# A conformer and attention layer: layer norm on rows between two sets of transposes, and softmax sums spread over partitions on chip

## The chip, the cores and the metric

The kernel runs on one core of a Trainium2 chip. Its engines are PE (TensorE, the matmuls), DVE (VectorE), ACT (ScalarE), POOL (GpSimd) and SP (SyncE, which here issues every DMA, one after the other). The metric is the device time of one execution in microseconds. Lower is better.

## The reference, cut to what matters

One layer is computed for 2048 prompt tokens and 32 tokens of running streams, all in fp32. Two parts of it matter here: the layer norm of the convolution branch, which takes a mean and a variance over the 512 channels of one token, and the softmax's division by the sum of its row.

```python
glu = a * jax.nn.sigmoid(b)
y = conv1d_depthwise(glu, conv_w) + conv_b        # width 31, causal, 512 channels
mu = mean(y, -1); var = mean((y - mu)**2, -1)     # per token
y = (y - mu) * rsqrt(var + EPS) * ln_g + ln_b     # ln_g, ln_b per channel
y_conv = silu(y) * silu(gate_c)
...
s = (q_nope @ k_nope.T + q_rope @ k_rope.T) * ATT_SCALE   # 8 heads, masked by chunks of 64
p = softmax(s, -1)
y_att = (p @ v) * silu(gate_a)                            # 64 channels a head
mixed = concat([y_conv, y_att], -1) @ w_out
return x + rmsnorm(mixed, g_post)
```

## The kernel before, in words

**Stages.** The program has three stages. Stage A (to about 507 us) brings x in, norms and transposes it and runs the input projection in two halves of 1024 tokens; half 1 carries the 32 stream tokens too. Every product is made of three matmuls, because each fp32 operand is split into a high and a low part (`emit_chunk`, L359 to L361: `xh,wh`, `xl,wh`, `xh,wl`; POOL makes the low part `wl` of each weight block at L156, and the raw blocks `wraw` are loaded on SP's queue). The convolution's 31 taps run beside it on DVE (L381) and on POOL with ACT. Stage B (to about 1090 us) is attention, stage C the output projection and the stream tokens' attention. Half 0's layer norm falls to the middle of stage A, between the two halves; half 1's falls to the start of stage B.

**Layout.** The result of the convolution, `acc`, lies with channels on partitions: 4 tiles of 128 channels by the tokens. A token's mean and variance run over partitions and tiles.

**Layer norm before.** For 128 tokens PE transposes four 128x128 blocks of `acc` into a PSUM tile `tp` (L198 in half 0, L1388 in half 1), DVE takes mean and variance of each row (L178, L179), and POOL turns the variance into 1/sqrt (L142, L143). The result `bmv` has two numbers a token, tokens on partitions. But `acc` has tokens along its rows, so each partition needs all tokens' numbers: SP stores `bmv` to DRAM (`st_d`, L185), and, after that has landed, loads it into all 128 partitions (`z<-st_d`, L187). Then two operations subtract and multiply (L193 on DVE for half 0, L149 on POOL for half 1). Half 0 ends with `emit_mix`: for each of the four channel tiles a Silu over 1024 tokens on ACT (L208), a gate load of 512 KB, a product on POOL and a store to `mix_d`. There are 8 such token tiles in half 0 and 9 in half 1 (the ninth has 32 rows).

**Softmax sums before.** The product of the unnormalised weights with v comes out as `yp`, channels (two heads of 64) on partitions. The reciprocal sums `rl` (L1163, L1164 on DVE) have queries on partitions. For each of 32 pairs of heads and 256 queries, `store_rl` stores the two heads' sums to DRAM (`rl_d`, L1280, 256 numbers of 4 B each), loads the gate (`gat`, L1288), and loads the sums back, each head's over 64 partitions (`rlb<-rl_d`, L1291, twice); POOL multiplies `gat` by `rlb`, then `yp` by `gat`, and the result goes to `mix_d` (L1306).

**What sets the order.** In stage A the Tile framework's scheduler orders what the program emits; the layer norm's steps are handed to a background queue (`later`, `bg`) with a cost of `LC` = 3 each, and `queue_ln` puts the second step of a tile `LL` = 2 tiles behind its first. In stage B a planner in the program keeps a clock for each engine (`hold`, `after`, `tps` for the PSUM tiles `tp`, with `DL` = 10 us assumed for a DMA) and writes the order of PE, ACT, DVE and POOL; that order is kept. SP's order is the scheduler's throughout. Each engine takes its instructions strictly in its order, and SP too: a DMA that must wait for another keeps all later ones waiting. Also on SP's queue in stage B are the stores and loads that stage k and v through DRAM (`k_d<-lng`, `v_d<-lng` from the staging tiles `lng` and `stgw`, which ACT fills from PSUM at L834; PE's products into `tp` for them are at L880) and the rotary tables (`tab`, L1022, used by DVE at L1053). PE's lines in attention are L1117 to L1119 (scores `sps`), L1202 to L1208 (transposes of the weights `pc`), L1253 to L1256 (`ops`, weights with v); `ql` is the low part of the queries, made by POOL at L156.

Of the kernel before, what the change touches and what calls it, by code (L numbers as in the profile page):

```python
# [88 lines left out]
def hybrid_stream_step(ctx: ExitStack, tc: tile.TileContext, a: dict, o: dict):  # L89
# [24 lines left out]
    rl_d = dram.tile([NH, SEQ], F32, name="rl_d")  # L114
# [46 lines left out]
    lnp = conv_ctx.enter_context(tc.tile_pool(name="lnp", bufs=4, side="left"))  # L161
# [3 lines left out]
    zs = {}  # L165
# [8 lines left out]
    def ln_stats(t, ps, r):  # L174
# [6 lines left out]
        return mv  # L181

    def ln_spread(t, mv, r):
        rows = st_d[t * P:t * P + r]
# [3 lines left out]
        return z  # L188

    def ln_apply(z, c0, r, subtract, multiply):  # L190
        x = acc[:, :, c0:c0 + r]
        for tt, op, q in ((subtract, ALU.subtract, 0), (multiply, ALU.mult, 1)):
            tt(x, x, z[:, :r, q].unsqueeze(1).broadcast_to([P, CT, r]), op)  # L193

    def emit_ln(t, c0, r):
        ps = ln_pool["ps"].tile([P, 512], F32, name="tp")
        for i in range(CT):
            nc.tensor.transpose(ps[:r, i * P:(i + 1) * P], acc[:, i, c0:c0 + r], ident)  # L198
        zs[t] = ln_spread(t, ln_stats(t, ps, r), r)

    def emit_ln2(t, c0, r):
        ln_apply(zs.pop(t), c0, r, nc.vector.tensor_tensor, nc.vector.tensor_tensor)

    def emit_mix(i, t0, n):
        g = lnp.tile([P, HALF + DEC], F32, name="lng", bufs=1)
        nc.sync.dma_start(out=g[:, :n], in_=gate_d[i, :, t0:t0 + n])
        y = acc[:, i, :n]
        nc.scalar.activation(y, y, AF.Silu, bias=col(LN_B, i), scale=col(LN_G, i))  # L208
        pool_tt(y, y, g[:, :n], ALU.mult)
        nc.sync.dma_start(out=mix_d[i, :, t0:t0 + n], in_=y)  # L210

    with ExitStack() as pa:
# [295 lines left out]
        for half in range(2):  # L508
# [77 lines left out]
            if half == 0:  # L586
                queue_ln([(j, j * P, P) for j in range(8)])
# [14 lines left out]
            for n, key in enumerate(seq2[:8 - len(lastpair)]):  # L602
# [7 lines left out]
                if half == 0 and n == CT - 1:  # L610
                    for i in range(CT):
                        later(lambda i=i: emit_mix(i, 0, HALF), LC)
            if lastpair:
# [7 lines left out]
                for ci, (c0, m) in enumerate(chunks):  # L621
# [5 lines left out]
                    if ci == 0:  # L627
                        transpose_x(range(8, 12), 0, fill=True)
# [11 lines left out]
    with ExitStack() as pb:  # L640
# [40 lines left out]
        def load_wkv():  # L681
            raw = lnp.tile([P, HALF + DEC], F32, name="lng", bufs=1)[:, 0:NH * P].rearrange("p (h c) -> p h c", h=NH)
# [140 lines left out]
        spare = lnp.tile([P, HALF + DEC], F32, name="lng", bufs=1)  # L823
        stgw = wk.tile([P, 1024], F32, name="stgw", bufs=1)
        stgs = [stgw[:, i * 512:(i + 1) * 512] for i in range(2)]
        stgs += [spare[:, i * 512:(i + 1) * 512] for i in range(2)]
# [244 lines left out]
        rows, rls = {}, {}  # L1071
# [28 lines left out]
        def s_run(ready):  # L1100
# [6 lines left out]
            if c == 0:  # L1107
                if j == 0:
                    rls[(h, g)] = small.tile([P, 2], F32, name="rl2", bufs=12)
                rt = small.tile([P, 8], F32, name="row", bufs=RB)  # L1110
                rows[(h, g, j)] = {"mx": rt[:, 0:4], "ls": rt[:, 4:8], "rl": rls[(h, g)][:, j:j + 1], "p": {}}
# [35 lines left out]
        def e_run(ready):  # L1147
# [10 lines left out]
            if c == ns - 1:  # L1158
                def total(ready):
# [6 lines left out]
                    if j:  # L1166
                        store_rl(h, g)
# [108 lines left out]
        def store_rl(h, g):  # L1276
            ts = slice(g * 256, (g + 1) * 256)

            def put(ready):
                nc.sync.dma_start(out=rl_d[h, ts].rearrange("(j p) -> p j", p=P), in_=rls.pop((h, g)))  # L1280
                t = hold("sp", 0.4, ready) + DL
                if h % 2:
# [495 lines left out]
```

## Time and profile before

| | |
|---|---|
| median of three runs | 1310.7 us (1310.13 to 1317.46) |
| the profiled execution | 1310.61 us, its span 1308.8 us |
| PE busy | 1232.9 us, 94% of the span |
| DVE, ACT, POOL busy | 883.0, 749.2, 627.2 us |
| granted PE clock, mean | 0.974 |
| DMA, mean | 95 GB/s, 42.2% of the 16 engines' time |

PE has little idle time in all, but it is not spread evenly: it lies where stages meet. A row of a view reads: start or total, length, engine, line of the kernel, operation, output<-inputs, and in brackets the idle time before it with the instruction or DMA that ended it. The granted clock is a share of full speed: 1.00 is 2.4 GHz, and a mean between .5 and 1 is a mix of 1.2 and 2.4 GHz.

### The profile page before, as it was taken

Reading aid. Unit: us, or ns where it says so; the run is one execution under the profiler, and the core shown is the slowest. Engines: PE = TensorE matmul, PEld = TensorE weight load, DVE = VectorE, ACT = ScalarE, POOL = GpSimd, SP = SyncE. Lnnn points to the kernel's source line nnn. Section 1 sums busy time; section 2 is a strip of 40 time slices with the busy share of each in tenths; the row PEclk is TensorE's granted clock in tenths of the full one; section 3 lists DMA queues with packets and bytes.
Section 4 is the critical chain, followed back from the end, with each engine's and each line's share of the span. In section 5 each row is a group of like instructions: output and inputs, shape, how many; then the busy total and the mean of one; then the engine's idle time right before and its main releaser. Section 6 shows DMA issues by size and latency. Waiting matters only on the chain.

```text
span 1308.8 us, 20918 instructions
## 1 busy us (share of the span) xinstructions
PE 1232.9 (94%) x7272; PEld 1100.1 (84%) x7272; DVE 883.0 (67%) x1814; ACT 749.2 (57%) x1748; POOL 627.2 (48%) x680
## 2 busy tenths in 40 slices
PE   7999999699999998868996999999999999999997
PEld 6889987589899997757896999999999998788876
DVE  4299898255997913646684888898988884543333
ACT  5366722155565223656685888888888884345221
POOL 5299942136999322545554434545554365111110
PEclk8999999899899999989998999999999999999999
DMA  8122253223313323596666323355245356944332
GB/s 294 31 72 80 79 140 105 56 57 109 113 49 87 113 83 91 107 117 123 115 76 92 37 44 43 76 58 63 46 79 47 39 90 132 284 156 144 95 109 69
DMA packets 166606, 124.23 MB, mean 95 GB/s; under 512 B 67031, under 2 KB 148489, under 8 KB 166499
## 3 DMA queue, kind: packets, MB, share of 16 engines
q1 hardware_dynamic: 166339, 122.82, 42.2%
q8 instruction: 57, 0.93, 0.4%
q14 instruction: 50, 0.41, 0.3%
q10 hardware_dynamic: 160, 0.07, 0.0%
HBM read 83.64 MB, written 39.21 MB: 94 GB/s over the span
## 4 chain that ended last, share of the span: by engine, by line
PE 71%; DMA 13%; DVE 6%; POOL 5%; ACT 3%; issue 2%; SPq 1%; POOLq 0%; DVEq 0%; ACTq 0%
PE mm L361 7%; PE mm L360 7%; PE mm L359 7%; PE sps L1117 4%; PE sps L1119 4%; PE sps L1118 4%; DMA st_d<-bmv 3%; PE ops L1255 2%; PE yx L1710 2%; PE yx L1711 2%; PE yx L1709 2%; DVE cv L381 2%; PE sps L1711 2%; PE sps L1710 2%; PE sps L1709 2%; PE mm L441 2%
## 5 line engine op out<-in xcount | busy, mean ns | idle before, releaser
L381 DVE SCALAR_TENSOR_TENSOR cv<-glu,cwT,cv 128x1024 f32<-128x1024 f32 x186 | 239.7, 1289 | 6.0
L1154 ACT ACTIVATE pc<-pc,row 128x512 f32<-128x512 f32 (+3 forms) x320 | 210.2, 659 | 34.3 <-DVE pc L1133 33.6
L360 PE MATMUL mm<-xl,wh 128*128 128x352 f32 (+1 forms) x584 | 209.2, 358 | 2.6 <-DVE xl L347 2.5
L361 PE MATMUL mm<-xh,wl 128*128 128x352 f32 (+1 forms) x584 | 208.0, 356 | 3.2 <-POOL wl L156 3.2
L359 PE MATMUL mm<-xh,wh 128*128 128x352 f32 (+1 forms) x584 | 208.0, 358 | 0.3 <-ACT xh L331 0.3
L1224 DVE TENSOR_TENSOR ptl<-tp,pth 128x512 fp32r<-128x512 f32 (+1 forms) x288 | 187.8, 656 | 28.9 <-ACT pth L1220 26.2
L1220 ACT CAST pth<-tp 128x512 fp32r<-128x512 f32 (+1 forms) x288 | 159.9, 558 | 35.0 <-PE tp L1208 24.7
L1133 DVE TENSOR_SCALAR_CACHE_REDUCE pc<-sps,row 128x512 f32<-128x512 f32 (+2 forms) x192 | 125.7, 655 | 21.8 <-PE sps L1119 14.6
L1117 PE MATMUL sps<-kh,qh 128*128 128x512 f32 (+3 forms) x320 | 132.8, 415 | 4.0 <-DVE pc L1133 2.6
L360 PEld LDWEIGHTS mm<-xl,wh 128*128 128x128 f32 x584 | 112.2, 192 | 13.8 <-DVE xl L347 3.9
L361 PEld LDWEIGHTS mm<-xh,wl 128*128 128x128 f32 x584 | 112.3, 192 | 13.3 <-POOL wl L156 3.5
L1119 PE MATMUL sps<-kh,ql 128*128 128x512 f32 (+3 forms) x320 | 116.7, 365 | 6.6 <-POOL ql L156 6.6
L359 PEld LDWEIGHTS mm<-xh,wh 128*128 128x128 f32 x584 | 112.4, 193 | 10.9 <-ACT xh L331 0.6
L149 POOL TENSOR_TENSOR acc<-acc,ptap 128x512 f32<-128x512 f32 x92 | 118.7, 1306 | 4.6 <-ACT acc L386 2.7
L1118 PE MATMUL sps<-kl,qh 128*128 128x512 f32 (+3 forms) x320 | 116.1, 363 | 0.0
L156 POOL TENSOR_TENSOR wl<-wraw,wh 128x1024 fp32r<-128x1024 f32 x27 | 64.9, 2403 | 97.6 <-ACT wh L155 97.5
L156 POOL TENSOR_TENSOR ql<-qf,qh 128x256 fp32r<-128x256 f32 x64 | 46.9, 735 | 114.0 <-ACT qh L155 98.8
L1255 PE MATMUL ops<-ptl,vb 128*128 128x256 f32 x288 | 85.9, 298 | 5.6 <-DVE rl L1163 4.4
L1253 PE MATMUL ops<-pth,vb 128*128 128x256 f32 x288 | 88.2, 306 | 2.2 <-ACT pth L1220 2.2
L149 POOL TENSOR_TENSOR yp<-yp,low 64x256 f32<-64x256 f32 x64 | 46.9, 734 | 89.2 <-ACT low L1264 88.1
L1133 DVE TENSOR_SCALAR_CACHE_REDUCE pc<-sps 128x512 f32<-128x512 f32 (+3 forms) x128 | 80.0, 628 | 12.8 <-PE sps L1119 11.2
L1202 PE MATMUL tp<-ident,pc 128*128 128x128 f32 x288 | 80.3, 279 | 6.6 <-ACT lng L834 4.9
(386 smaller groups left out, 3265.2 us busy)
## 6 DMA issues: line engine op xcount, KB each, us to landing
wraw<-in_w_in SPq DMA_DIRECT2D x31, 512.0 KB
xr<-in_x_prompt SPq DMA_DIRECT2D x16, 512.0 KB
out_y_p<-src SPq DMA_DIRECT2D x32, 256.0 KB
mix<-mix_d SPq DMA_DIRECT2D x7, 1024.0 KB
gate_d<-gt SPq DMA_DIRECT2D x24, 176.0 KB
xt<-in_x_prompt SPq DMA_DIRECT2D x8, 512.0 KB
gate_d<-gt SPq DMA_DIRECT2D x16, 256.0 KB
gat<-gate_d SPq DMA_DIRECT2D x32, 128.0 KB
```

The source lines that it names most:

```text
L149: nc.gpsimd.tensor_tensor(dst, x, y, op)
L359: nc.tensor.matmul(ps[:, :n], wh[:, k], rh, start=(k == 0), stop=False)
L360: nc.tensor.matmul(ps[:, :n], wh[:, k], rl, start=False, stop=False)
L361: nc.tensor.matmul(ps[:, :n], wl[:, k], rh, start=False, stop=(k == KT - 1))
L381: nc.vector.scalar_tensor_tensor(box["ps"], x, cw(j), box["ps"], ALU.mult, ALU.add)
L1117: nc.tensor.matmul(d, qh[:, qs], kh[b][:, ks], start=True, stop=False)
L1118: nc.tensor.matmul(d, qh[:, qs], kl[b][:, ks], start=False, stop=False)
L1119: nc.tensor.matmul(d, ql[:, qs], kh[b][:, ks], start=False, stop=True)
L1133: nc.vector.tensor_scalar(p_[:, :m], d, -SCALE, r["mx"][:, c - 1:c] if c else None, ALU.mult, ALU.min, accum_out=r["mx"][:, c:c + 1])
L1154: nc.scalar.activation(p_, p_, AF.Exp, bias=r["mx"][:, ns - 1:ns], scale=-1.0, accum_out=r["ls"][:, c:c + 1])
L1220: nc.scalar.copy(out=ph[:, :nn], in_=ps[:, :nn])
L1224: nc.vector.tensor_tensor(pl[:, :nn], ps[:, :nn], ph[:, :nn].bitcast(F32), ALU.subtract)
```

## The change

**Layer norm.** The tile's rows in PSUM, tokens on partitions, are normed right there: a DVE `tensor_scalar` reads `tp` and subtracts and multiplies with the row's own two numbers, into the place of the tile in `acc`, now as rows. Four more transposes (`ln_back`, L196 after) bring it back to channels on partitions in a second `tp` tile. From there half 0 goes through Silu on ACT straight from PSUM (four of 128x128 a tile, in place of four of 128x1024 for all), a POOL product of 128x512 with a gate tile of two slots, and one store a tile; half 1 goes through one ACT copy of 128x512 and the store. `st_d` and `z` are gone: 17 stores and 17 loads. `queue_ln` is now called after half 0's gates, and not ahead of its latents, a tile's second step stands ahead of the next one's first, and the transposes of x for tiles 8 to 11 take their PSUM from `mm`, not from `tp`.

**Softmax sums.** The sums of two heads and 256 queries are gathered in one tile `rlt`. POOL widens them to 128x256 (each sum copied 64 times along the row), PE transposes that in two 128x128 pieces (L1296), so that the sums lie along rows on the right partitions, and DVE multiplies them from PSUM with the gate (L1300). POOL's product with `yp` is as before. Gone are 64 stores `rl_d`, 64 loads `rlb` and 32 products on POOL.

```diff
 def queue_ln(jobs):
     for i in range(len(jobs) + LL):
+        if i >= LL:
+            later(lambda a=jobs[i - LL]: emit_ln2(*a), LC)
         if i < len(jobs):
             later(lambda a=jobs[i]: emit_ln(*a), LC)
-        if i >= LL:
-            later(lambda a=jobs[i - LL]: emit_ln2(*a), LC)
...
-def ln_spread(t, mv, r):
-    nc.sync.dma_start(out=rows, in_=mv[:r])
-    z = lnp.tile([P, P, 2], F32, name="z")
-    nc.sync.dma_start(out=z[:, :r], in_=rows.partition_broadcast(P))
-def ln_apply(z, c0, r, subtract, multiply):
...
+def ln_rows(ps, c0, r):
     nc.vector.bn_stats(st[:r], ps[:r])
     nc.vector.bn_aggr(mv[:r], st[:r])
     rsqrt_eps(mv[:r, 1:2], mv[:r, 1:2], 1)
+    x = ln_x(c0, r)
+    nc.vector.tensor_scalar(x, ps[:r].rearrange("p (k c) -> p k c", k=CT), mv[:r, 0:1], mv[:r, 1:2],
+                            ALU.subtract, ALU.mult)
+def ln_back(ps, c0, r):
+    x = ln_x(c0, r)
+    for i in range(CT):
+        nc.tensor.transpose(ps[:, i * P:i * P + r], x[:, i], ident[:r, :r])
...
-            if half == 0:
-                queue_ln([(j, j * P, P) for j in range(8)])
             latents(half, tiles)
...
-                    for i in range(CT):
-                        later(lambda i=i: emit_mix(i, 0, HALF), LC)
+                    queue_ln([(j, j * P, P) for j in range(8)])
...
-                        transpose_x(range(8, 12), 0, fill=True)
+                        transpose_x(range(8, 12), 0, mm, fill=True)
...
-            nc.sync.dma_start(out=rl_d[h, ts].rearrange("(j p) -> p j", p=P), in_=rls.pop((h, g)))
-                nc.sync.dma_start(out=rb[i * VD:(i + 1) * VD], in_=rl_d[h - 1 + i, ts].partition_broadcast(VD))
+                pool_copy(rb, rlt[h // 2 % 2][:, g].unsqueeze(3).broadcast_to([P, 2, 2, VD]))
+                nc.tensor.transpose(ps[:, j * P:(j + 1) * P], rb[:, j], ident)
-                pool_tt(gt, gt, rb, ALU.mult)
+                nc.vector.tensor_tensor(gt, ps[:, 0:256], gt, ALU.mult)
```

On DVE, at the third layer-norm tile of half 0 and the transposed x that follows (`xl`), the order before is:

```order
61 L193 TENSOR_TENSOR acc<-acc,z 128x4x128 [waits DMAHW2_49]
62 L193 TENSOR_TENSOR acc<-acc,z 128x4x128 [waits DVE_49]
63 L178 BN_STATS bst<-tp 128x6 [waits PE_49]
64 L193 TENSOR_TENSOR acc<-acc,z 128x4x128 [waits DMAHW4_49]
65 L179 BN_AGGR bmv<-bst 128x2 [waits DVE_49]
66 L193 TENSOR_TENSOR acc<-acc,z 128x4x128 [waits DVE_49]
67 L332 SCALAR_TENSOR_TENSOR xl<-tp,cols,xh 128x512 [waits Activation_49]
```

and now, from the first tile on:

```order
56 L182 BN_STATS bst<-tp 128x6 [waits PE_49]
57 L183 BN_AGGR bmv<-bst 128x2 [waits DVE_49]
58 L186 TENSOR_SCALAR acc<-tp,bmv 128x4x128 [waits DVE_49,Pool_49]
59 L182 BN_STATS bst<-tp 128x6 [waits PE_49]
60 L183 BN_AGGR bmv<-bst 128x2 [waits DVE_49]
61 L333 SCALAR_TENSOR_TENSOR xl<-mm,cols,xh 128x512 [waits Activation_49]
62 L186 TENSOR_SCALAR acc<-tp,bmv 128x4x128 [waits DVE_49,Pool_49]
63 L333 SCALAR_TENSOR_TENSOR xl<-mm,cols,xh 128x512 [waits Activation_49] x3
```

The two operations with `z`, each pair behind a DMA, have become one operation behind POOL's 1/sqrt, in a chain of DVE and POOL alone.

On SP, early in attention, between the load of a block of latents (`src<-ckv_d`) and the staging stores that follow it, the order before is:

```order
222 L185 DMA st_d<-bmv 128x2 [waits DMAHW4_49,DVE_49,Pool_49]
223 L774 DMA src<-ckv_d 128x4x128 [waits DMAHW5_49,PE_49]
224 L187 DMA z<-st_d 128x256 [waits DMAHW6_49,DMAHW4_49]
225 L1280 DMA rl_d<-rl_4762 128x2x1 [waits DMAHW7_49,DVE_49]
226 L775 DMA src<-kr_d 128x4x64 [waits DMAHW0_49]
227 L860 DMA k_d<-lng 128x512 [waits DMAHW1_49,Activation_49]
228 L782 DMA src<-qn_d 128x4x256 [waits DMAHW2_49,PE_49]
229 L185 DMA st_d<-bmv 128x2 [waits DMAHW3_49,DVE_49,Pool_49]
230 L886 DMA v_d<-lng 128x512 [waits Activation_49]
```

and at the same loads now:

```order
209 L772 DMA src<-ckv_d 128x4x128 [waits DMAHW5_49,PE_49]
210 L773 DMA src<-kr_d 128x4x64 [waits DMAHW6_49]
211 L1412 DMA mix_d<-acc 128x4x128 [waits DMAHW7_49,Activation_49]
212 L857 DMA k_d<-lng 128x512 [waits DMAHW0_49,Activation_49]
213 L780 DMA src<-qn_d 128x4x256 [waits DMAHW1_49,PE_49]
214 L883 DMA v_d<-lng 128x512 [waits DMAHW2_49,Activation_49]
```

The rows with `st_d`, `z` and `rl_d` are gone from between the loads and `k_d`, and a store `mix_d<-acc`, which waits for ACT, stands there.

On PE, in attention, at the same scores of one unit (`sps`, 384 keys) and the same products with v, the order before is:

```order
3957 L1205 MATMUL tp<-ident,pc_6315 128x128
3958 L1117 MATMUL sps_4391<-kh_4421,qh 128x384 [waits DVE_49]
3959 L1118 MATMUL sps_4391<-kl_4423,qh 128x384
3960 L1119 MATMUL sps_4391<-kh_4421,ql 128x384
3961 L1253 MATMUL ops_4458<-pth,vb_4424 128x256 [waits Activation_49]
3962 L1254 MATMUL ops_4458<-pth,vb_4424 128x256
```

and now:

```order
4010 L1201 MATMUL tp<-ident,pc_4471 128x128
4011 L1113 MATMUL sps_4435<-kh_4465,qh 128x384 [waits DVE_49]
4012 L1114 MATMUL sps_4435<-kl_4467,qh 128x384
4013 L1115 MATMUL sps_4435<-kh_4465,ql 128x384
4014 L1296 MATMUL tp<-ident,rlb 128x128 [waits PE_49,Pool_49]
4015 L1296 MATMUL tp<-ident,rlb 128x128
4016 L1249 MATMUL ops_4502<-pth,vb_4468 128x256 [waits Activation_49]
4017 L1250 MATMUL ops_4502<-pth,vb_4468 128x256
```

The two transposes of the widened sums `rlb` stand between them, and wait for POOL. Of the 32 pairs of them 8 stand in the part of the order that belongs to attention's start (to 725 us in the trace before), the other 24 behind it.

## Rows read from the trace of the kernel before

**Rows 1.** By stage: length, PE, PEld, DVE, ACT, POOL busy us, clock, DMA share, GB/s

```profile
215.00:345.00 130.00, 110.53 (x608) 100.31 (x608) 70.38 (x91) 51.97 (x85) 60.17 (x56) 0.91 0.32 87
505.00:725.00 220.00, 182.24 (x1147) 159.64 (x1146) 136.54 (x399) 139.45 (x345) 112.36 (x157) 0.94 0.64 104
725.00:1080.00 355.00, 353.89 (x2570) 332.73 (x2569) 313.24 (x969) 304.96 (x805) 170.14 (x183) 1.00 0.41 57
```

**Rows 2.** Waits of PE from 215 to 345 us: total, times, longest us

```profile
PE tp L330 <- DVE xl L332: 5.6, 2, 3.8
PE tp L330 <- DVE bst L178: 5.4, 2, 3.1
PE mm L361 <- POOL wl L156: 3.2, 1, 3.2
```

**Rows 3.** Waits of DVE from 215 to 345 us

```profile
DVE acc L193 <- DMA z<-st_d: 41.9, 7, 8.5
```

**Rows 4.** Waits of SP's queue from 215 to 345 us

```profile
SPq L187 <- DMA st_d<-bmv: 28.5, 7, 6.7
```

**Rows 5.** Waits of PE from 505 to 725 us

```profile
PE sps L1119 <- POOL ql L156: 6.6, 2, 5.2
PE tp L1202 <- ACT lng L834: 4.9, 3, 4.2
PE ops L1255 <- DVE rl L1163: 4.4, 1, 4.4
PE tp L880 <- ACT lng L834: 4.3, 1, 4.3
PE tp L880 <- ACT stgw L834: 2.4, 2, 1.2
```

**Rows 6.** SP's instructions in order of time, around 550 us

```profile
543.43 0.37 SPq L774 DMA_DIRECT2D src<-ckv_d  x1
552.00 0.32 SPq L187 DMA_DIRECT2D z<-st_d  x1
553.40 0.45 SPq L860 DMA_DIRECT2D k_d<-lng  x1
```

**Rows 7.** PE's in order of time, around 565 us: start, length, [idle before]

```profile
565.38 0.47 PE L1202 MATMUL tp<-ident,pc 128*128 128x128 f32 x1 [4.24 <-ACT lng L834]
```

**Rows 8.** 20 us of the attention's start, columns as in the first group

```profile
560.00:580.00 20.00, 11.18 (x55) 8.85 (x55) 6.08 (x22) 9.41 (x25) 8.57 (x15) 0.74 0.80 145
```

**Rows 9.** PE's in order of time, around 227 us

```profile
226.39 0.39 PE L361 MATMUL mm<-xh,wl 128*128 128x512 f32 x1
226.62 0.60 PE L198 MATMUL tp<-ident,acc 128*128 128x128 f32 x4
226.98 0.47 PE L359 MATMUL mm<-xh,wh 128*128 128x512 f32 x1
227.29 0.39 PE L360 MATMUL mm<-xl,wh 128*128 128x512 f32 x1
```

**Rows 10.** PE's in order of time, around 802 us

```profile
801.68 0.27 PE L1202 MATMUL tp<-ident,pc 128*128 128x128 f32 x1
...
802.00 0.27 PE L1208 MATMUL tp<-ident,pc 128*128 128x128 f32 x1
```

**Rows 11.** Groups by line and form: busy us, mean ns | idle before

```profile
L1053 DVE TENSOR_TENSOR qf<-tp,tab 128x256 f32<-128x256 f32 x62 | 26.2, 423 | 30.0 <-DMA tab<-in_rope_q 10.7 <-POOL ql L156 6.6 <-PE tp L1046 4.6
L149 POOL TENSOR_TENSOR gat<-gat,rlb 128x256 f32<-128x256 f32 x32 | 24.6, 770 | 32.0 <-DMA gat<-gate_d 17.1 <-DMA rlb<-rl_d 9.1 <-issue 5.8
L156 POOL TENSOR_TENSOR wl<-wraw,wh 128x1024 fp32r<-128x1024 f32 x27 | 64.9, 2403 | 97.6 <-ACT wh L155 97.5
L834 ACT COPY lng<-tp 128x512 f32<-128x512 f32 x16 | 9.4, 589 | 14.4 <-DMA k_d<-lng 8.4 <-DMA v_d<-lng 3.4 <-PE tp L856 1.8
```

**Rows 12.** POOL's in order of time, around 582 us

```profile
581.95 0.23 POOL L142 TENSOR_SCALAR bmv<-bmv 128x1 f32<-128x1 f32 x1 [0.70 <-DVE bmv L179]
582.26 0.57 POOL L143 TENSOR_TENSOR bmv<-bmv,nhalf 128x1 f32<-128x1 f32 x1
```

More of the change, by code (lines that the diff above doesn't have):

```diff
@@ L681, in load_wkv @@
         def load_wkv():
-            raw = lnp.tile([P, HALF + DEC], F32, name="lng", bufs=1)[:, 0:NH * P].rearrange("p (h c) -> p h c", h=NH)
+            raw = lng[:, 0:NH * P].rearrange("p (h c) -> p h c", h=NH)
             nc.sync.dma_start(out=raw, in_=w_kvb.rearrange("p (h c) -> p h c", h=NH))
@@ L821, in prep_tasks @@
                     (lambda: latest(box["t2"], tps.ready()), query(1))]
-        spare = lnp.tile([P, HALF + DEC], F32, name="lng", bufs=1)
         stgw = wk.tile([P, 1024], F32, name="stgw", bufs=1)
         stgs = [stgw[:, i * 512:(i + 1) * 512] for i in range(2)]
-        stgs += [spare[:, i * 512:(i + 1) * 512] for i in range(2)]
+        stgs += [lng[:, i * 512:(i + 1) * 512] for i in range(2)]
         stg = Slots(len(stgs))
@@ L1070, in hybrid_stream_step @@
         banks, pcs, gats = Slots(NB), Slots(NP), Slots(2)
-        rows, rls = {}, {}
+        rows = {}
+        rlt = [small.tile([P, 8, 2, 2], F32, name=f"rlt{i}", bufs=1) for i in range(2)]
         exp_q = []
@@ L1274, in pv_run, with scale_rows @@
                 after("act", PE_["ot"], t, out)
[L1276 removed]
+        def scale_rows(h, g):
             ts = slice(g * 256, (g + 1) * 256)
[L1279 to L1283 removed]
+            if h % 2 == 0:
+                return
             def load(ready):
@@ L1307, in save @@
                     done[("mix", h, g)] = hold("sp", 0.4, ready) + DL
-                after("pool", PE_["gate"], t, scale)
-            after("sp", PE_["gate"], latest(done[("rl", h, g, 0)], done[("rl", h, g, 1)]), put)
+                after("dve", PE_["gate"], t, scale)
+            after("sp", PE_["gate"], lambda: gats.ready(), load)
         q_list = list(range(len(units)))
@@ L1386, in l_run, with back, out @@
             ps = tp.tile([P, 512], F32, name="tp")
-            for i in range(CT):
-                nc.tensor.transpose(ps[:r, i * P:(i + 1) * P], acc[:, i, c0:c0 + r], ident)
+            ln_turn(ps, c0, r)
             te = hold("pe", t_pe(256, 4), ready)
-            zk = zslots.take()
             def stats(ready):
-                mv = ln_stats(t, ps, r)
-                te = hold("dve", t_dve(512) + 0.1, ready)
+                ln_rows(ps, c0, r)
+                te = hold("dve", t_dve(512) + 0.2, ready)
+                te = hold("pool", 0.3, te)
+                te = hold("dve", t_dve(512), te)
                 tps.give(kslot, te)
-                te = hold("pool", 0.3, te)
-                z = ln_spread(t, mv, r)
-                def norm(ready):
-                    ln_apply(z, c0, r, pool_tt, pool_tt)
-                    te = hold("pool", 2.4, ready)
-                    zslots.give(zk, te)
+                after("pe", PE_["l"], lambda: latest(te, tps.ready()), back)
+            def back(ready):
+                k = tps.take()
+                ps = tp.tile([P, 512], F32, name="tp")
+                ln_back(ps, c0, r)
+                te = hold("pe", t_pe(256, 4), ready)
+                def out(ready):
+                    nc.scalar.copy(out=acc[:, :, c0:c0 + r], in_=ps.rearrange("p (k t) -> p k t", k=CT)[:, :, 0:r])
+                    te = hold("act", t_act(512), ready)
+                    tps.give(k, te)
                     nc.sync.dma_start(out=mix_d[0:CT, :, HALF + c0:HALF + c0 + r].rearrange("k p t -> p k t"),
```

71 lines of the change are left out of this document (37 added, 34 removed).

## The prediction

> **What bounds the kernel now.** I read the busy times by stage first, then the waits of PE in the stages where it idles, then followed each wait back to the engine or queue that caused it. PE is busy for 94% of the span, so time can be won only where PE is not busy or where its clock is low, and every instruction that is added to PE elsewhere costs its full length. [Rows 1] say where: from 215 to 345 us, where the halves of stage A meet, PE is busy for 110.53 of 130 us, at a mean clock of 0.91; from 505 to 725 us, the start of attention, for 182.24 of 220 at 0.94; from 725 to 1080 us for 353.89 of 355 at 1.00.
>
> So the two stages offer 130.00 - 110.53 = 19.5 us and 220.00 - 182.24 = 37.8 us of idle time. The clock adds to it. A mean of 0.91 between 1.2 and 2.4 GHz is 18% of 130 us at the lower level, 23.4 us; PE is busy for 85% of the stage, and half of that is lost: 23.4 x 0.85 / 2 = 9.9 us. In attention's start 12% of 220 us is 26.4 us, and x 0.83 / 2 = 10.9 us. The fall of the clock goes with the idle time: in the emptiest 20 us PE is busy for 11.18 us at 0.74 [rows 8]. Together 29.4 us at the boundary and 48.7 us at the start.
>
> What PE waits for at the boundary is DVE: 5.6 and 5.4 us for the low part of the transposed x and for the statistics [rows 2], and DVE itself stood for 41.9 us, seven times, before operations with `z` [rows 3], whose load SP could issue only when the store of `bmv` had landed (28.5 us of SP's queue) [rows 4]. The 3.2 us for POOL's `wl` are of another kind. At attention's start the five largest waits of PE make 22.6 us [rows 5]. One of them can be followed through: SP issues a load at 543.43, stands behind `st_d` until it issues `z` at 552.00, and only then, at 553.40, the store `k_d<-lng` [rows 6]; ACT can't refill `lng` before that store has landed, and PE stands 4.24 us until 565.38 for ACT's copy [rows 7]. The other waits for `lng` and `stgw` are of this form; those for `ql` and `rl` hang on tables and gate loads that SP issued late, behind `rlb`.
>
> **The change, part by part.** *The layer norm's round trips*, 17 stores and 17 loads, go, and with them the 41.9 us of DVE. Of the 14.2 us of PE's waits in [rows 2], 3.2 stay with POOL; so about 70% of the 29.4 us, 20 us, is what could be won at the boundary. I take 18, since the new operation on DVE still waits, now for POOL's 1/sqrt, and behind it stand the statistics of the next tile and the `xl` that PE needs. The trace has no such wait, but its parts: in attention POOL begins as DVE's result comes and is done 0.9 us later (581.95 to 582.83) [rows 12]; at the boundary it can stand behind one `wl` of 2.4 us [rows 11]. Eight tiles make 8 x 0.9 = 7 us to 8 x (0.9 + 2.4) = 26 us of DVE's waiting, against 41.9. With all 26, two fifths of the gain stay, 18 x (1 - 26/41.9) = 7 us: that is the lower bound, and I take the value nearer to 0.9, the measured row.
>
> *Transposes added to the layer norm.* At 226.62 four of them run; the next two matmuls start 0.36 and 0.31 us later, and matmuls of 128x512 follow each other by 0.23 ahead of them [rows 9]: 0.36 + 0.08 = 0.44 us for four. Half 0 adds 8 x 0.44 = 3.5 us, half 1 adds 9 x 0.44 = 4.0.
>
> *Work of the others at the boundary.* DVE loses one of two operations a tile, POOL none that counts (four products of 128x1024 become eight of 128x512), SP's half-0 stores become eight of a tile. They wait for POOL's product, and the next raw weights stand behind them on SP; PE's margin there is the weights' lead, and the 3.2 us for `wl` may grow. I leave it at zero in the sum, with 0 to +6 us (two waits of 3.2) for the range. That x's transposes take PSUM from the ring of the projection can cost PE a wait for an eviction, or win one; it is in the same bounds.
>
> *Attention's start.* `z` and `rl_d`, `rlb` leave SP's queue. The 22.6 us of [rows 5] needn't vanish: staging through DRAM stays, the store `mix_d<-acc` now stands ahead of `k_d` and waits for ACT, which must first copy a tile (0.59 us each by the copies to `lng`, 9 x 0.59 = 5.3 us more on ACT, which is not full) [rows 11]. I take three quarters, 17 us, and of the clock the same share as of the idle time, 10.9 x 17 / 37.8 = 4.9: 22 us. Against it stand the 4.0 us of half 1's transposes and 8 of the 32 pairs that spread the sums. A transpose follows the one before by 0.32 / 3 = 0.107 us [rows 10], so a pair is 0.21 us, and 8 make 1.7.
>
> *The rest of attention.* The other 24 pairs are 24 x 0.21 = 5.1 us on a PE that has 1.1 us to spare [rows 1]: full price. That SP no longer stands for `rl_d` there wins nothing, since PE doesn't idle for it. DVE takes over the product with the gate at 0.42 us (by `qf`, which also reads PSUM [rows 11]), 24 x 0.42 = 10 us on top of 313 of 355: no bound yet. POOL gives up 0.77 us and takes a widening copy of similar size. The 17.1 us that POOL waited for `gat` [rows 11] become DVE's, if they stay; DVE makes weights that PE waits for, so here the bounds are 0 and +6 us (a third of 17.1). I take 0, because the gate load no longer stands behind `rl_d`.
>
> Sum: boundary -18 + 3.5 = -14.5; start -22 + 4.0 + 1.7 = -16.3; rest +5.1. That is -25.7 on the profiled 1310.6 us, which is the median of the runs too (1310.7): **1285 us**.
>
> **The rivals.** *The transfers are late anyway.* The DMA engines are busy for 0.80 of the emptiest 20 us [rows 8] and for 0.64 of the whole start [rows 1]. If their load, and not SP's blocked queue, makes the staged tiles late, only the waits for `ql` and `rl` behind the tables and the gate go, three quarters of 6.6 + 4.4 = 11.0, 8 us: start -8 + 5.7 = -2.3, and in all -14.5 - 2.3 + 5.1 = -11.7, 1299 us. With the lower bound at the boundary as well (-7 + 3.5) it is -0.7, 1310. For it: the load. Against it: the 8.6 us between two issues in [rows 6], which no load of the engines explains. The Trainium skill, "DMA: Bandwidth & Descriptors", section "Issuing engines are not separate DMA queues", says that all DMAs end up on the same 16 engines; that speaks for this rival, and no row here tells how much of the busy share is the many small packets that leave.
>
> *New waits on PE: the slower side.* PE gets 17 + 32 = 49 places at which its strict order waits for a chain of DVE and POOL that was not in its way before: 1/sqrt or widening on POOL, with its operations of 0.7 to 2.4 us. If PE stood there for 0.9 us each time (POOL's part in [rows 12]), it would lose 44 us, and the time would be 1285 + 44 = 1329. It breaks even at 25.7 / 49 = 0.52 us a place, and is slower by 1% from 0.79 us. Against it: PE waits today on POOL's `ql` at every unit, and from 725 to 1080 us it idles for 1.1 us in all, with POOL busy for less than half of the time [rows 1]; the back transposes stand a tile or more behind.
>
> *All of it is won.* If the boundary's 20 us and nine tenths of the start's 48.7 go, it is -20 + 3.5 - 44 + 5.7 + 5.1 = -50, 1261 us. Against it: attention's start also has to load its first k and v through DRAM, whoever issues.
>
> *The transposes run at the lower clock.* From 725 to 1080 us, where transposes of the weights stand between all products, the granted clock is 1.00 [rows 1], and they follow each other by 0.107 us [rows 10]. If the added ones brought the clock down around themselves, their 14.3 us would count twice: 1285 + 14 = 1299. The Trainium skill, "TensorE: Matmul & The Clock Gate", section "Part 4: PE-mode transpose", says that a transpose doesn't count as busy for the clock; this trace speaks against an effect of it here.
>
> **How the numbers follow.** A measurement of this kernel tells about 1% from no change, so the bounds are 1297.6 and 1323.8 us. My forecast, with a spread of some 12 us from its two recovered terms, has 0.50; all of it won 0.10; transfers late anyway 0.25; lower clock 0.03; new waits on PE 0.12. Faster by over 1% is the forecast and the full gain with a little of the third, 0.63; within 1% most of the third, the fourth and a little of the slower side, 0.27; slower 0.10. The range must hold 8 in 10: it reaches from 1264, near the full gain, to 1310, the third case with its lower bound and +6 us for `wl`; outside are the slower side and the end of the full gain.
>
> **What would show it.** Right: no idle time of DVE at the boundary above 3 us; PE idle for under 8 us there; SP with gaps of 1 to 3 us, not 8, before `k_d<-lng`; PE's waits for `lng` and `stgw` below 4 us in all; 64 transposes of `rlb` without a wait; the stage from 725 us some 5 us longer for the same work. Wrong: a PE wait for `lng` as long as before with a DMA share of 0.8 (transfers), or waits of PE at L196 and L1296 that sum to over 15 us (new waits).

## The result, and the profile after

The changed kernel takes **1263.29 us** (median of four runs, 1261.26 to 1267.61), the kernel before 1310.95 beside it: a ratio of 0.963, with a 95% interval from 0.959 to 0.967. The forecast was 1285 us, and its range, 1264 to 1310, missed the time by 0.7 us. The direction was right, and the gain 47.7 us in place of 25.7. The profiled execution of the changed kernel took 1267.61 us, the longest of the four, so the traces explain 43.0 us and the other 4 to 5 lie in runs that were not profiled. In a second group the changed kernel came to 1262.1 us and the kernel before to 1299.75: the gain there is 37.7 us. The direction holds in both groups; the size of the gain hangs on the kernel before, which varies more.

Where the time went is read from instructions that are the same in both kernels. The first column of the table is the last `xh,wh` matmul of stage A's projection (L359 before, L360 after), the next ones the 101st and the last score matmul of attention (L1117 before, L1113 after), each by its start in the trace:

| | projection ends | 101st score | last score | span |
|---|---|---|---|---|
| before | 506.4 | 741.6 | 1078.7 | 1308.8 |
| after | 485.4 | 698.9 | 1038.7 | 1265.8 |
| difference | -21.0 | -42.7 | -40.0 | -43.0 |

So 21.0 us are won by the end of stage A (all of it before 350 us, where the halves meet), another 21.7 in attention's start, 2.7 are lost in the rest of attention, and 3 are won behind it. The stages of the changed kernel, cut at the same work as in [rows 1] (length, busy us of PE, PEld, DVE, ACT, POOL, clock, DMA share, GB/s):

```profile
215.00:324.00 109.00, 105.56 (x642) 98.56 (x641) 71.50 (x85) 62.27 (x115) 64.55 (x62) 0.98 0.31 91
484.00:683.00 199.00, 182.51 (x1206) 161.91 (x1205) 144.95 (x415) 144.54 (x354) 90.70 (x142) 0.97 0.36 107
683.00:1039.00 356.00, 356.00 (x2604) 335.50 (x2602) 318.58 (x990) 304.65 (x804) 166.94 (x185) 1.00 0.19 52
```

The boundary has 3.4 us of idle PE in place of 19.5, at a clock of 0.98; attention's start 16.5 in place of 37.8, at 0.97; the stretch behind it none. The DMA engines' share fell from 0.64 to 0.36 in the start and from 0.41 to 0.19 behind it.

At the boundary PE's waits, with [rows 2] beside them, are:

```profile
PE tp L176 <- DVE acc L409: 1.9, 1, 1.9
PE mm L331 <- DVE xl L333: 1.1, 1, 1.1
PE mm L360 <- DVE xl L333: 0.3, 1, 0.3
```

The 1.9 us are for the end of the convolution, as before. DVE, which stood for 41.9 us [rows 3], now stands for POOL's 1/sqrt, six times, 2.4 at most:

```profile
DVE acc L186 <- POOL bmv L142: 7.2, 6, 2.4
```

SP's queue stands there still, but for POOL's product ahead of the store and for `wl`, and PE doesn't feel it:

```profile
SPq L211 <- POOL acc L148: 28.3, 7, 14.8
SPq L254 <- POOL wl L155: 23.8, 3, 14.0
```

In attention's start, SP's instructions at the place of [rows 6], in order of time:

```profile
524.01 0.38 SPq L772 DMA_DIRECT2D src<-ckv_d  x1
525.49 0.36 SPq L1412 DMA_DIRECT2D mix_d<-acc  x1
528.20 0.33 SPq L857 DMA_DIRECT2D k_d<-lng  x1
```

The store of `k_d` follows the load by 4.2 us in place of 10.0, and a store of normed rows stands between. PE's largest waits there, where [rows 5] made 22.6 us:

```profile
PE tp L196 <- DVE acc L186: 3.4, 3, 2.1
PE tp L788 <- issue: 3.2, 2, 1.8
PE ops L1249 <- ACT pth L1216: 1.6, 2, 0.8
```

For `lng` PE stood 11.2 us in the start before: two of the lines are in [rows 5], the third is

```profile
PE tp L1044 <- ACT lng L834: 2.0, 1, 2.0
```

Now it is 0.3 us, 0.2 for the sums, and nothing for `stgw` and `ql`. The new operations, by line and form (busy us, mean ns, idle before):

```profile
L1300 DVE TENSOR_TENSOR gat<-tp,gat 128x256 f32<-128x256 f32 x32 | 13.4, 420 | 8.2 <-PE tp L1296 7.9
L186 DVE TENSOR_SCALAR acc<-tp,bmv 128x512 f32<-128x512 f32 x16 | 13.0, 810 | 15.8 <-POOL bmv L142 15.6
L145 POOL TENSOR_SCALAR rlb<-rlt 128x256 f32<-128x256 f32 x32 | 12.6, 405 | 0.2
L1296 PE MATMUL tp<-ident,rlb 128*128 128x128 f32 x64 | 12.2, 273 | 0.0
L196 PE MATMUL tp<-ident,acc 128*128 128x128 f32 x64 | 10.5, 286 | 3.5 <-DVE acc L186 3.4
```

DVE's product with the gate takes 0.42 us, as priced; in the whole run DVE stood 8.2 us ahead of it and 15.8 us ahead of the rows' operation; the transposes of `rlb` never kept PE waiting.

### The profile page after: what moved, and what is told of

Its sections match the earlier page's. It is cut to its first block, busy times and chain, and to the rows that moved or that the text cites. A ratio compares the mean times of both kernels' runs of the same rounds, so it can differ in the third digit from the quotient of the medians.

```text
span 1265.8 us, 21060 instructions
## 1 busy us (share of the span) xinstructions
PE 1229.1 (97%) x7404; PEld 1104.1 (87%) x7404; DVE 892.8 (71%) x1847; ACT 763.5 (60%) x1787; POOL 596.1 (47%) x666
## 4 chain that ended last, share of the span: by engine, by line
PE 89%; DVE 5%; ACT 2%; POOL 1%; DMA 1%; issue 1%; SPq 0%; DVEq 0%; POOLq 0%; ACTq 0%
PE mm L360 9%; PE mm L361 9%; PE mm L362 9%; PE sps L1113 5%; PE sps L1114 5%; PE sps L1115 5%; PE ops L1251 3%; PE ops L1249 3%; PE tp L1198 2%; PE tp L1199 2%; PE ops L1252 2%; PE ops L1250 2%; DVE cv L382 2%; PE yx L1718 2%; PE yx L1720 2%; PE sps L1720 2%
## 5 line engine op out<-in xcount | busy, mean ns | idle before, releaser
L360 PE MATMUL mm<-xh,wh 128*128 128x352 f32 (+1 forms) x584 | 205.8, 354 | 0.7 <-DVE xl L333 0.3
L361 PE MATMUL mm<-xl,wh 128*128 128x352 f32 (+1 forms) x584 | 205.5, 352 | 0.0
L362 PE MATMUL mm<-xh,wl 128*128 128x352 f32 (+1 forms) x584 | 204.6, 351 | 0.0
L1113 PE MATMUL sps<-kh,qh 128*128 128x512 f32 (+3 forms) x320 | 132.3, 414 | 1.7 <-DVE pc L1129 0.7
L360 PEld LDWEIGHTS mm<-xh,wh 128*128 128x128 f32 x584 | 110.4, 189 | 11.1 <-ACT xh L332 0.6
L391 ACT ACTIVATE ptap<-glu,cwT 128x512 f32<-128x512 f32 x92 | 65.8, 723 | 36.8 <-POOL acc L148 36.4
```

The costliest lines, as they stand in the source:

```text
L360: nc.tensor.matmul(ps[:, :n], wh[:, k], rh, start=(k == 0), stop=False)
L361: nc.tensor.matmul(ps[:, :n], wh[:, k], rl, start=False, stop=False)
L362: nc.tensor.matmul(ps[:, :n], wl[:, k], rh, start=False, stop=(k == KT - 1))
L1113: nc.tensor.matmul(d, qh[:, qs], kh[b][:, ks], start=True, stop=False)
```

## The experiments

All are edits of the changed kernel, where nothing else is said, and are compared with the runs of the kernel before in their own group. That kernel's median ranges from 1296.4 to 1321.0 us between the groups, while the changed kernel came out at 1263.3 and, in a second group, at 1262.1; so edits of the changed kernel are compared by absolute time and by marks in the traces. The kernel before was traced once, and its marks carry that spread: a difference against them is known to some 10 us, a difference between two edits better. The marks of all runs:

| run | median us | projection ends | 101st score | last score |
|---|---|---|---|---|
| changed kernel, twice | 1263.3, 1262.1 | 485.4, 485.3 | 698.9, 695.9 | 1038.7, 1035.7 |
| ln_only | 1280.5 | 485.4 | 705.4 | 1041.9 |
| sums_only | 1276.8 | 503.0 | 706.7 | 1046.8 |
| trips | 1503.5 | 496.0 | 775.8 | 1270.4 |
| trips_free | 1334.5 | 485.8 | 728.1 | 1104.6 |
| st_only | 1267.3 | 484.3 | 698.8 | 1038.9 |
| ld_only | 1265.2 | 482.9 | 694.2 | 1037.9 |
| sum_free | 1319.9 | 484.3 | 712.0 | 1090.3 |
| sum_trips | 1307.3 | 485.1 | 708.1 | 1078.4 |
| half0_sums | 1255.4 | 484.7 | 686.5 | 1026.6 |
| late_ln | 1273.8 | 484.3 | 704.2 | 1042.7 |
| split | 1259.9 | 484.9 | 691.5 | 1031.3 |
| x_tp | 1263.6 | 484.2 | 695.0 | 1034.7 |
| spread4 | 1269.5 | 485.1 | 698.5 | 1043.2 |
| dl6 | 1250.9 | 485.3 | 686.7 | 1026.6 |
| split_dl6 | 1243.1 | 485.3 | 680.7 | 1020.6 |
| half0_dl6 | 1242.5 | 483.0 | 676.8 | 1016.7 |
| before_dl6 | 1340.8 | 501.7 | 744.1 | 1102.7 |

**The two parts, each alone.** `ln_only` is the kernel before with the layer norm's edits, `sums_only` with the edits to the softmax's sums.

```diff
 ln_only:   +ln_rows, ln_back, emit_ln2, l_run as changed;  store_rl, rl_d, rlb as before
 sums_only: +scale_rows, rlt, spread as changed;  ln_spread, st_d, z, emit_mix, l_run as before
```

> The layer norm's part alone; the softmax's sums go through DRAM as before. Measured for the whole change: the boundary of the halves 21 us shorter, the start of attention 21 to 22 us shorter net, the rest within 3 us. If the two parts add, this one has the boundary's 21 us and about half of the start's, no cost in the rest: 1310 - 21 - 11 = 1278 us, range 1272 to 1284. Rival, the start is won only when both kinds of round trip are off SP's queue: the boundary alone, 1287 to 1293 us.

> The softmax sums' part alone; the layer norm goes through DRAM as before. If the parts add: nothing at the boundary, about 11 us of the start, and +2 to +5 us in the rest: 1300 to 1304 us. Rival, the start is won only with both parts: 1312 to 1316 us, slower than before by the added transposes.

Measured: `ln_only` 0.9695 (0.9656 to 0.9733) of the kernel before in its group, 1320.97 us, and `sums_only` 0.9672 (0.964 to 0.9705). By absolute time `ln_only`, 1280.5 us, lies in its range and `sums_only`, 1276.8, far below its own; the sum that both rested on failed. Each part alone wins some 40 to 44 us in its group, and by the traces 34 to 35 of the 43; the two don't add. The marks say why. The boundary belongs to the layer norm alone (485.4). From there to the 101st score the kernel before takes 235.2 us, `ln_only` 220.0, `sums_only` 203.7, and both together 213.5: in attention's start the sums' part wins 31.5 us by itself, and the layer norm's part, put on top, gives back 9.8 (6.9 by the second trace of the changed kernel). The layer norm's part alone wins 15.2. Before, SP stands in the start for both kinds of round trip, and for `st_d` alone 45.1 us:

```profile
SPq L187 <- DMA st_d<-bmv: 45.1, 9, 8.1
```

In `sums_only` it still does so nine times:

```profile
SPq L186 <- DMA st_d<-bmv: 33.4, 9, 6.9
```

and yet the waits that PE had for `lng` are all but gone:

```profile
PE tp L1200 <- ACT lng L833: 0.6, 2, 0.3
PE ops L1251 <- ACT pth L1218: 2.2, 2, 1.8
PE sps L1117 <- POOL ql L155: 1.4, 1, 1.4
PE tp L1201 <- ACT pc L1152: 1.1, 1, 1.1
```

`ln_only` is the reverse. SP still stands for the sums,

```profile
SPq L1289 <- DMA rl_d<-rl: 22.8, 4, 13.3
```

and PE's waits for `lng` are 0.6 us there too. Added up from the end of stage A to the 101st score, SP stands for landings for 104 us before, 42 in `sums_only`, 40 in `ln_only` and 2 in the changed kernel. So the landings of `st_d`, which the prediction followed through [rows 6] to [rows 7], do not make PE's waits for `lng` by themselves, and the sums' trips don't either; both together did, and do again in `trips` below.

**Dead round trips.** To see whether it is SP's standing, the traffic or the data itself, the trips are put back with no reader. In `trips_free`, `ld_only` and `sum_free` the loads read an input and wait for no store. In these three and in `sum_trips` a tiny write of DVE into the tile `zx` holds the loads to their places, which has a price of its own, below; `trips` has no such write.

```diff
 trips:
+        nc.sync.dma_start(out=st_d[rows], in_=mv[:r])                     # 17
+        nc.sync.dma_start(out=zx[:, :96], in_=st_d[rows].partition_broadcast(P))
+            nc.sync.dma_start(out=rl_d[h, ts]..., in_=rlt[h // 2 % 2][:, g, :, h % 2])   # 64
+            nc.sync.dma_start(out=rx[...], in_=rl_d[h - 1 + i, ...].partition_broadcast(VD))  # 64
 trips_free:
+        nc.vector.memset(zx[:, 0:1, 0:1], 0.0)
-        ... in_=st_d / rl_d            +        ... in_=a["x_prompt"][0, k, ...]
```

> The changed kernel with the round trips put back on SP's queue as dead weight: 17 stores of the statistics and 17 loads that wait for them, 64 stores of the sums and 64 loads that wait for them (192 columns in place of 256), into a tile that nobody reads. The order of PE, DVE, ACT and POOL is that of the changed kernel, word for word. Theory, the start of attention was lost to SP's queue standing behind landings (or to the traffic): the start gives back most of its 21 us, the boundary little, since DVE reads nothing of it there: 1280 to 1290 us. Rival, the loss was DVE and POOL waiting for the data themselves: within 4 us of the changed kernel, 1263 to 1268 us.

> The same transfers in number and size, but the loads read an input tensor and wait for nothing that is on its way (a tiny write of DVE holds each to its place). If SP's queue standing behind landings is what cost the start: near the changed kernel, 1263 to 1270 us. If the traffic on the DMA engines is the cost: as slow as the run with the waits, 1280 us or more.

Measured: `trips` 1503.5 us, far beyond what either theory gave, and `trips_free` 1334.5. At the boundary `trips` ends stage A 10.6 us later, with every engine but SP in the changed kernel's order, and SP standing there as it did before:

```profile
SPq L192 <- DMA st_d<-bmv: 37.1, 8, 6.7
```

`trips_free`, with the same transfers and no waits for them, ends stage A at 485.8. So 10.6 of the 16 to 21 us of the boundary's gain are SP's queue free of landings. The rest, which doesn't come back, is what `trips` leaves changed: DVE no longer reads `z`, and the steps stand in a new order; the two were not separated. In attention's start, where SP again stands for landings for 133 us, PE's waits for `lng` are back, 7.2 us in all:

```profile
PE tp L179 <- ACT lng L839: 4.7, 1, 4.7
PE tp L1206 <- ACT lng L839: 2.5, 3, 1.7
```

In the later part of attention SP stands for the stores of the sums,

```profile
SPq L1292 <- DMA rl_d<-rlt: 228.4, 28, 9.8
```

and behind them on its queue are the gate loads and the rotary tables, for which DVE now stands in its strict order,

```profile
DVE gat L1319 <- DMA gat<-gate_d: 69.1, 9, 33.1
DVE qf L1058 <- DMA tab<-in_rope_q: 68.1, 8, 16.5
```

and PE behind DVE, at the very transposes that the change added (L1315 here):

```profile
PE tp L1315 <- DVE gat L1319: 41.2, 2, 31.3
```

In the kernel before it was POOL that stood for the late gate (17.1 us [rows 11]), and DVE went on. The change thus makes PE depend on prompt gate loads. It costs nothing in the changed kernel, which also empties SP's queue.

`trips_free` loses 71 us, although its loads wait for no store. Four more runs take the sums' trips alone, apart and together.

```diff
 st_only:   the 64 stores rl_d                  ld_only:   the 64 free loads, held by DVE's tiny write
 sum_free:  both, loads from x_prompt           sum_trips: both, loads from rl_d, DVE's tiny write too
```

> The changed kernel with the 64 stores of the sums alone put back (256 numbers of 4 B each, nobody reads them); all engines but SP in the changed kernel's order. The run with stores and free loads lost 70 us. If the small packets of the stores, or SP standing for DVE ahead of each, is the cost: 20 us or more slower than the changed kernel. If it is the loads: within 5 us.

> The changed kernel with 64 loads alone (64 partitions x 768 B, from an input tensor, each held to its place by a tiny write of DVE). If the loads' traffic or their waits are the cost of that run: 20 us or more slower than the changed kernel. If the stores: within 5 us.

> The changed kernel with the sums' 64 stores and 64 loads both as dead weight (the layer norm's trips left away), the loads from an input tensor, so that no load waits for its store; order and places on SP's queue are those of the next run. Each half by itself cost nothing measurable (1267 and 1265 us in one run each). If the transfers add up on the DMA engines: 1280 us or more. If only a queue that stands for a landing costs: 1263 to 1272 us.

> The same, row for row, except that the loads read what the stores wrote, so that SP stands until each store has landed. If the standing is the cost: 1300 us or more, with waits of SP for rl_d of over 100 us and PE waiting for DVE behind gat. If the transfers are: as the run before.

Measured: `st_only` 1267.3 and `ld_only` 1265.2, one run each, so no cost that these can tell. Together 1319.9 us without a wait between store and load, and 1307.3 with it. From 690 to 1040 us the stores alone raise the DMA engines' share from 0.19 to 0.35, at the same 53 GB/s, and PE is as busy as without them:

```profile
690.00:1040.00 350.00, 349.92 (x2558) 329.67 (x2558) 312.99 (x970) 299.71 (x791) 165.93 (x184) 1.00 0.35 53
```

The loads alone land after 2.6 us, and DVE's tiny write, which waits for the load before it, stands 2.2 us at most:

```profile
zx<-in_x_prompt SPq DMA_DIRECT2D x64, 48.0 KB, 2.6
DVE zx L1166 <- DMA zx<-in_x_prompt: 5.4, 3, 2.2
```

With the stores among them they land late; DVE stands up to 8.7 us in `sum_free`,

```profile
DVE zx L1166 <- DMA zx<-in_x_prompt: 33.4, 7, 8.7
```

which PE pays:

```profile
690.00:1040.00 350.00, 330.54 (x2354) 308.26 (x2353) 287.19 (x917) 274.80 (x725) 143.02 (x163) 0.98 0.33 47
```

In `sum_trips` SP stands up to 8.7 us for a store, but DVE's write stands just as in `sum_free`:

```profile
SPq L1288 <- DMA rl_d<-rlt: 39.0, 6, 8.7
DVE zx L1166 <- DMA zx<-rl_d: 29.1, 6, 8.6
```

From 640 us to the last score every wait of PE over 4 us, three in `sum_trips` and four in `sum_free`, ends 0.7 to 0.8 us after this write has stood for 6 to 9 us. So both runs price a wait of DVE, my own holder, and neither the traffic nor SP's standing; the comparison of the two decides nothing between the theories. That SP's standing can cost, `trips` shows, which has no holder and where SP stood for `rl_d` for 228.4 us in place of 39.0. What these runs do show is that with stores of 256 numbers of 4 B around, a wait for a load reached 8.7 us, against 2.2 without them, and that the stores alone, when nobody on PE's path waits for a landing, cost nothing that one run can tell.

**Half 1's layer norm.** Three edits ask why the rows give back 7 to 10 us in attention's start. `split` also tells the planner of 0.9 us, not 0.3, for POOL's 1/sqrt.

```diff
 half0_sums: l_run, ln_stats, ln_spread, ln_apply and four z tiles for half 1 as before
 late_ln:   -BS = 0     +BS = 40
 split:     -   ln_rows(ps, c0, r)                  # statistics, 1/sqrt, subtract and multiply in a row
            +   mv = ln_rows(ps, c0, r, True)       # statistics and 1/sqrt
            +   after("dve", PE_["ln"], te, norm)   # subtract and multiply as a step of its own
```

> The changed kernel with the layer norm of half 1 alone put back: through DRAM, as before. In the profiled runs the sums' part alone made the stretch from the end of stage A to the end 31 us shorter, both parts together 22 us; so the layer norm on rows in half 1 costs about 9 us there. If that holds, this kernel is 8 to 10 us faster than the changed one: a ratio to the kernel before of 0.955 to 0.958, with the boundary of the halves still 21 us shorter. Rival, the two runs differed by a chance meeting in the order: within 3 us of the changed kernel, 0.961 to 0.965.

> The changed kernel with half 1's layer norm started 40 steps of attention later, behind the start (about 640 us and on) in place of in it; the same work, the same engines. If the 9 to 12 us that half 1's layer norm on rows costs are work and waits put where PE, DVE and ACT are in each other's way (the start): 5 to 10 us faster than the changed kernel, 1254 to 1259. If it is the work itself (36 transposes, 9 copies, 9 operations of DVE): within 3 us of it.

> The changed kernel with half 1's layer norm split in the planner on DVE: the statistics, and then, as a step of its own that is due when POOL should have the 1/sqrt, the subtract and multiply. Between them DVE takes other work in place of standing for POOL (9.4 us in nine waits in the changed kernel's attention start). If that standing is what half 1's rows cost, it is passed on to PE: 5 to 10 us faster than the changed kernel. If the cost is the work itself (PE, DVE and ACT take what POOL did): within 3 us of it.

> The changed kernel once more, as the yardstick on the chip of this group. Absolute time 1261 to 1268 us as before, whatever the kernel before shows on this chip.

Measured: `half0_sums` 1255.4 us, 7 to 8 below the changed kernel and 8 below `x_tp`, which has the layer norm on rows too and ran in the same group: the theory's 8 to 10, nearly. (Its ratio, 0.968 to a kernel before of 1296.4, can't be held against the expected one.) `late_ln` 1273.8: that expectation failed. Without the rows the start is indeed shorter, the 61st score comes at 620.9 in place of 636.3 us; but where the rows now stand, the way from the 61st to the 101st score takes 83.3 us in place of 62.6. There PE idles for 9 of 80 us and DVE is busy for 65:

```profile
620.00:700.00 80.00, 70.98 (x496) 63.51 (x496) 65.06 (x191) 53.61 (x139) 35.01 (x50) 0.98 0.24 66
```

`split` takes 1259.9 us against 1262.1 in its own group. DVE's standing for POOL in the start, in the changed kernel

```profile
DVE acc L186 <- POOL bmv L142: 9.4, 9, 1.2
```

and in `late_ln`

```profile
DVE acc L186 <- POOL bmv L142: 10.4, 9, 2.3
```

is gone from the start in `split`, and 2 us are won: every run of `split` (1259.31 to 1260.71) is below every run of the changed kernel beside it (1261.37 to 1264.42). So the standing is the smaller part. The larger, by elimination, is work: the rows put 36 transposes (4 us) on PE, 9 operations of 0.81 us on DVE and 9 copies on ACT into a stretch where these three pass weights to each other, in place of 18 operations on POOL, which had room. This wasn't shown by a run of its own; how the rest divides between them wasn't tried, nor was 1/sqrt on DVE itself.

**Two prices.** `x_tp` takes back the other PSUM ring for the transposes of x; `spread4` doubles the transposes that spread the sums, writing the extra ones where nobody reads.

```diff
 x_tp:    -transpose_x(range(8, 12), 0, mm, fill=True)   +transpose_x(range(8, 12), 0, fill=True)
 spread4: -for j in range(2):   +for j in (2, 3, 0, 1):  # rb[:, j % 2]
```

> The changed kernel with the transposes of x for tiles 8 to 11 in the layer norm's PSUM ring again (tp, two tiles). The prediction had put the move to the other ring at nothing. If it is nothing: the boundary still 21 us shorter, ratio 0.963. If a good part of the boundary's gain is the ring (the waits of PE before stood at these transposes): the boundary gives back 4 us or more, ratio 0.966 or above.

> The changed kernel with four transposes for each of the 32 pairs in place of two (the two extra ones write a part of the PSUM tile that nobody reads). All else in the same order. By the price of the prediction, 0.21 us for two, the 24 pairs after the start cost 5 us and all 32 cost 7 us: ratio 0.968 to 0.969. If they fit into slack of PE: under 2 us.

Measured: `x_tp` 1263.6 us, stage A's end 1.2 us earlier than in the changed kernel: the ring is worth nothing. `spread4` 1269.5 us, 6 to 7 more; from the 101st to the last score 344.7 us against 339.8. Of the 32 pairs 22 stand there (8 ahead, 2 behind), so 22 more cost 4.9 us, 0.22 each.

**The planner's DMA time.** With 10 us assumed for a DMA, steps behind one are put late.

```diff
-DL = 10.0
+DL = 6.0
```

> The changed kernel with the planner's assumed DMA time at 6 us in place of 10, since the queue is emptier now. If attention's start is still set by where the planner puts the steps behind a DMA: 3 to 8 us faster. If PE's order then runs ahead of the data: slower by as much. If the start is bound otherwise: within 3 us.

> The split and the planner's DMA time at 6 us. If both win and add as half 1's DRAM path and the 6 us did (1242.5 us): 1240 to 1246 us. If the split wins nothing: 1249 to 1253 us, as the 6 us alone.

> Both edits that helped: half 1's layer norm through DRAM, and the planner's DMA time at 6 us. They won 11.7 and 16.8 us of the profiled run. If they win at different places, 1242 to 1247 us; if both shorten the same waits of attention's start, 1249 to 1252.

> The kernel before with the planner's DMA time at 6 us. If the gain from it comes from the emptier queue of the change: here nothing, or slower, since landings took 4 to 9 us with SP's queue full: ratio 0.998 or above. If it is an error of the plan in either kernel: 5 to 15 us faster, ratio 0.988 to 0.996.

Measured: 1250.9 us on the changed kernel, beyond the 3 to 8 us expected, 1243.1 with the split and **1242.5** with half 1's layer norm through DRAM, the lowest median, at 0.958 (0.9553 to 0.9608) of the kernel before in its group; the runs of the last two overlap. So the edits add. On the kernel before the same number loses 3.2% (1.032, 1.0275 to 1.0364). By the traces the start is 7 us longer and the way from the 101st to the last score 21.5 (358.6 us against 337.1). By PE's waits the order there runs ahead of the data; in the start:

```profile
PE sps L1119 <- POOL ql L156: 16.7, 3, 8.5
PE tp L880 <- ACT lng L834: 8.3, 1, 8.3
PE sps L1117 <- DVE pc L1133: 6.1, 2, 5.8
```

The attention of `half0_dl6`, start and rest:

```profile
482.00:662.00 180.00, 172.87 (x1173) 156.25 (x1172) 139.47 (x409) 140.39 (x347) 112.26 (x160) 0.99 0.48 124
662.00:1017.00 355.00, 355.00 (x2596) 334.51 (x2595) 317.72 (x985) 304.55 (x799) 170.09 (x187) 1.00 0.18 52
```

Of the start's 16.5 us of idle PE 7.1 are left.

## Why the prediction was wrong

*Boundary, -18 + 3.5.* The mechanism was right, and the term a little small. The trace shows -21.0, but 3 to 5 us of that are the profiled run of the kernel before: `sums_only` and `before_dl6`, with the same stage A, end it at 503.0 and 501.7, not 506.4. Against these it is 16 to 18 us where I had 14.5. I had held back 2 of the 20 us for DVE's waits for POOL, between 7 and 26 us; they came out at 7.2. The 20 itself was low: 11.0 of the 14.2 us of PE's waits are 77%, 22.8 us, not 70%. What the prediction didn't separate, and `trips` does: 10.6 us of it are SP's queue.

*Attention's start, -22 + 4.0 + 1.7.* This is the step that failed: the price of the emptied queue, and of the rows. The chain from SP's standing to PE's waits for `lng` was there: they fell from 11.2 to 0.3 us, and `trips` brings 7.2 back. But I took one sum for both kinds of round trip, 17 of the 22.6 us that PE's five largest waits made and a share of the clock, and put the other 15 of the 37.8 us of idle time at nothing without a reason. `sums_only` alone wins 31.5 us there, known to some 10 us, so about the whole term or more, with the stores and loads of `z` still in place; `ln_only` alone wins 15.2, net of its rows. Either one ends the waits for `lng`, so the wait that I followed could not price the two. Why the sums' part is worth so much stays open: its stores, its loads, POOL's wait for them and the planner's order, which counts one DMA fewer in that chain, all go at once. Put back as dead weight into the changed kernel, the sums' trips give 9.5 us of the start (`sum_trips`, 223.0 against 213.5), DVE's holder included. The second size is the layer norm's rows in half 1: 4.0 us for transposes in the sum; measured by `half0_sums` 7 to 8 us, and in the traces 7 to 12. I had priced PE's part of the exchange and called ACT and DVE not full, which is true over the stage; what the chain from scores to weights loses by them was left out.

*The rest of attention, +5.1.* `spread4` measures 0.22 us a pair, where I had 0.21. But the stretch grew by 2.7 only. `ln_only`, which has no spreading transposes, takes 336.5 us there, `before` 337.1, and the changed kernel 339.8. Twenty-two pairs make 4.8 us; PE's idle time in that stretch went from 1.1 us to none, and where the other 1 us went isn't shown.

*The sum.* By the traces these three stretches differ from the forecast by -6.5, -5.4 and -2.4 us, and 3.0 us more were won behind the last score (230.1 us before, 227.1 after), which I had at nothing and no run explains: 17.3 us in all. The other 4 to 5 us of the miss lie in runs that were not profiled.

*The rivals.* Transfers late anyway: no, PE's waits for `lng` fell to 0.3 us and the DMA engines' share in the start to 0.36. The load may have had a part: SP stood 5.0 us a time for `st_d` before and 3.7 in `sums_only`; the traces of these kernels don't show when the sums' stores landed. New waits on PE, the slower side: not in the changed kernel, where PE waited 3.4 us at L196 and never at L1296; but `trips`, with SP's queue full again, shows the mechanism at the transposes of `rlb` with 41.2 us. All of it won: closest in time at 1261, by luck, since it has 38 us for the start, where 21.7 came and 16.5 us of idle time are still there. Transposes at the lower clock: no, from the 101st to the last score, with 22 of the 32 pairs, the granted clock is 1.00, and in `spread4` with twice as many too. The Trainium skill, "TensorE: Matmul & The Clock Gate", section "Part 4: PE-mode transpose", says that transposes don't count as busy for the clock in the same way; no effect of that shows in these two traces.

*The signs.* Of those named for being right, these came: PE's idle time at the boundary, 3.4 us; its waits for `lng` and `stgw`, 0.3; none at the transposes of `rlb`; 2.7 us between two issues of SP ahead of `k_d`. DVE's longest wait at the boundary is 3.9 us, not below 3, but for the convolution's `glu` and not for the layer norm.

## What to carry to other kernels

A wait that a trace shows behind one queued transfer doesn't price that transfer: here either of two kinds could go, and the wait went. Take each kind away by itself before adding the two up. A dead load that must be held to its place is not free: ask in the trace who waits for the holder. A round trip through DRAM that an idle engine waits for can be cheaper, by 7 to 8 us here, than the same work on three engines that wait for each other, and when a change empties a queue, a planner's assumed DMA time has to be measured again: here that was worth as much as a quarter of the change.

## What the runs showed that I had not expected

64 stores of 1 KB raised the DMA engines' share over 350 us from 0.19 to 0.35, while the same number of loads of 48 KB raised it to 0.21. Alone neither moved the time by an amount that one run can tell; together, with DVE held for the loads, they cost 45 to 57 us. And the same number in the planner, 6 us for a DMA, wins 12 us in one kernel and loses 41 in the other.
